# A whole program's instruction order, fixed by a plan in the kernel instead of by the scheduler

## Chip, cores, metric

One core of a Trainium2 chip runs the kernel. The metric is the device time of one execution in microseconds (us). The engines are the TensorE (PE in the profile; PEld is its weight load), the VectorE (DVE), the ScalarE (ACT), GpSimd (POOL) and the SyncE (SP), whose queue issues the DMA transfers.

## What is computed

The reference is a trunk of two layers over 512 tokens of width 1024. Each layer is a feed-forward part, a mixer and another feed-forward part:

```python
x = x + 0.5 * swiglu_ffn(rmsnorm(x, ffn1_norm[l]), ffn1_w_in[l], ffn1_w_out[l])
h = rmsnorm(x, mix_norm[l])
u_rwkv, u_gla, u_xa, u_gate = split_cols(h @ w_in[l], (RWKV_COLS, GLA_COLS, XA_WIDTH, GATE_COLS))
y_rwkv, v_first = rwkv7_mixer(u_rwkv, v_first, ...)
y_gla = gla_mixer(u_gla, gla_conv[l], gla_a_up[l], gla_a_bias[l], gla_norm[l])
y_xa = memory_attention(u_xa, rmsnorm(mem, mem_norm[l]), xa_w_kv[l])
branches = jnp.stack([y_rwkv, y_gla, y_xa], axis=2)
gates = jax.nn.sigmoid(u_gate.reshape(b, s, N_BRANCH, d))
merged = jnp.einsum('bsjc,jcd,bsjd->bsd', branches, w_branch[l], gates)
x = x + merged @ w_out[l]
x = x + 0.5 * swiglu_ffn(rmsnorm(x, ffn2_norm[l]), ffn2_w_in[l], ffn2_w_out[l])
```

The RWKV-7 mixer has 8 heads of width 64 and a state that each token updates: `state * w + sa * (kk * a) + v * k`, read out by `r`; its output is normalised per head, gets a bonus term and is multiplied by a gate. The gated linear attention has 4 heads in chunks of 64 tokens. The memory attention has 4 heads of width 128 over 256 memory rows.

## The kernel before

**Products.** Activations lie with features on the 128 partitions and the 512 tokens along the free axis. Every large product is made of three matmuls in fp32r for each 128 rows of its depth (`mm3`, L194 to L198; L307 in the mixer): weight and activation are split into a high and a low part, and high·high, high·low and low·high are summed in PSUM. Weights come from DRAM as `wraw` (L191, three buffers); the ScalarE rounds them to `whi` (L180), the VectorE makes `wlo` as the difference (L181). PSUM has three buffers `ps_b` for large products, and `ps_f` (one), `ps_i` (two), `ps_c` (one) and `ps_y` (one) for small ones. All small products are plain fp32.

**Stages of a layer.** The first feed-forward part (L262), then `mix` (L999): `xa_proj` projects the memory to keys and values, `norm_mix` (L218) makes the normalised `h` (`xn` at L226, its split `xhi`, `xlo` at L203 and L204); two of the four cross-attention heads; two pairs of GLA heads (`gla_pair`, which waits at L905 for the decays `gq` of L901); then the RWKV part; then branch 0, `w_out` (L1054 to L1061) and the second feed-forward part.

**The RWKV part** works on four pairs of heads (`hp`) by two halves of the tokens (`hf`), eight units in all. A unit consists of `rwkv_gates` and `rwkv_first` (vectors, masked products `MA` and `A4`, L459 and L472), `rwkv_inverse` (a triangular inverse by doubling, products `X` at L539 and `W` at L547 in turn), `rwkv_second` (the recurrence over chunks: L590 gives `qs`, L596 gives `VU`, L602 gives the new state `S`, and at the end L618 gives `y`) and `rwkv_out` (statistics of `y` down to L650, L655, the gate at L656, the result at L663 or L666). The last pair of heads leaves its result in `y3`, which branch 0 needs. The small products of these steps are a chain over TensorE, VectorE and ScalarE; the large products of the gates and branches, and of cross-attention heads 2 and 3, are put between them.

**What sets the order.** A scheduler that comes with the language orders all engines by priority, the program's order being the default. Two places differ. In `weave` (L670 to L778) the TensorE's order is written by hand (L1046): each part is a generator that yields the cost of the products it has just issued and the time until its next step is ready, and a loop takes the first part in a fixed list that is ready, or else a piece of the large products; all other engines are still left to the scheduler there, and the parts run under a raised priority. And `norm_mix` has a priority that is raised over everything else (L1011).

Of the kernel before, what the change touches and what calls it, by code (L numbers as in the profile page):

```python
# [19 lines left out]
P = 128  # L20
# [58 lines left out]

class Net:  # L80
    def __init__(self, ctx, tc, I):
        self.tc, self.nc, self.I = tc, tc.nc, I
        self.ctx = ctx
# [9 lines left out]
    def pool(self, name, bufs, ctx=None, **k):  # L93
        return (ctx or self.ctx).enter_context(self.tc.tile_pool(name=name, bufs=bufs, reuse_waits="tile", **k))
# [99 lines left out]
    def mm3(self, ps, a, b, start, stop):  # L194
        nc = self.nc
        nc.tensor.matmul(ps, a[0], b[0], start=start, stop=False)  # L196
        nc.tensor.matmul(ps, a[0], b[1], start=False, stop=False)  # L197
        nc.tensor.matmul(ps, a[1], b[0], start=False, stop=stop)  # L198

# [95 lines left out]
    @staticmethod  # L295
    def drain(g):
        while True:
            try:
                next(g)
            except StopIteration as e:  # L300
                return e.value

    def pieces(self, ps, w, xs):
        n = len(w)
        for k in range(n):
            for i, (a, b) in enumerate(((0, 0), (0, 1), (1, 0))):
                self.nc.tensor.matmul(ps, w[k][a], xs[k][b], start=k + i == 0, stop=k == n - 1 and i == 2)  # L307
                yield 227

    def proj_g(self, i):  # L310
        w = self.weight(self.I["w_main"][self.l, i], KD, P)
        ps = self.big()
        yield from self.pieces(ps, w, self.h)
        return ps

    def proj(self, i):
        return self.drain(self.proj_g(i))

    def shifted_g(self, i, out):

        nc = self.nc
        ps = yield from self.proj_g(i)
# [3 lines left out]

    def shifted(self, i, out):
        self.drain(self.shifted_g(i, out))
# [21 lines left out]
    def rwkv_rkv(self, hp):  # L350
# [16 lines left out]
        yield from self.shifted_g(4 + hp, k)  # L367
        r = self.lr.tile([P, T], F32, name="rk_r", tag="rk_r", bufs=1)
        yield from self.shifted_g(hp, r)
# [4 lines left out]

    def rwkv_gates(self, hp, hf, wz, r, k, v):
# [3 lines left out]
        if hf == 0:  # L381
# [5 lines left out]
            yield 0, 1800  # L387
# [22 lines left out]
        yield (2 * 432 if hf else 4 * 432), 6500  # L410
        return r, k, v, kk, kh, a, G

    def rwkv_first(self, hp, hf, r, k, v, kk, kh, a, G):
# [30 lines left out]
        yield 218, 4000  # L444
# [36 lines left out]
        self.freed = 2 * hp + hf + 1  # L481
        yield 8 * 218, 3600
# [23 lines left out]
        out = E, AR, VU, u0, GR, Z  # L506
        yield 8 * 116 + 432, 2800

        self.inv[2 * hp + hf] = Z, AB, AU, W32

        while self.tails < 2 * hp + hf - 1:
            yield None
# [5 lines left out]
        yield 4 * 109, 1000  # L518
# [4 lines left out]
        yield 432, 1000  # L523
        self.sec[2 * hp + hf] = (*out, KBT, bv)

    def rwkv_inverse(self, Z, AB, AU, W32):
# [8 lines left out]
        for b in (4, 8, 16):  # L535
# [8 lines left out]
            yield 4 * 216, 1000  # L544
# [4 lines left out]
            yield 4 * 216, 1300  # L549
# [12 lines left out]
        yield 432, 2100  # L562
# [8 lines left out]
        yield 432, 1300  # L571

    def rwkv_second(self, hp, hf, E, AR, VU, u0, GR, Z, KBT, bv):
# [4 lines left out]
        for c in range(4):  # L578
# [9 lines left out]
            else:  # L588
# [4 lines left out]
                yield 218, 650  # L593
# [5 lines left out]
            yield 218, 900  # L599
            if g < 7:  # L600
# [9 lines left out]
                if c < 3:  # L610
                    yield 218, 1000
# [12 lines left out]
        self.out[2 * hp + hf] = y, bv  # L624
        yield 5 * 218, 0

    def rwkv_out(self, hp, hf, y, bv):
# [23 lines left out]
        yield 0, 11000, 100000  # L651
# [16 lines left out]
        yield 218 + 432, 1500  # L668

    def weave(self, rkv0, gl, restore, xa):  # L670


        now, slack = 0, 400
        ready, rkv, gated, query = {0: 6000}, {0: rkv0}, {}, {}
        self.inv, self.sec, self.out, inverted = {}, {}, {}, 0
        self.freed = self.seconds = self.tails = 0

        def first_gates():
            for n in range(8):
                while n // 2 not in rkv or ready[n // 2] > now or self.freed < n:  # L680
                    yield None
                gated[n] = yield from self.rwkv_gates(n // 2, n % 2, *rkv[n // 2])

        def first():
            for n in range(8):
                while n not in gated or self.seconds < n - 1:
                    yield None
                yield from self.rwkv_first(n // 2, n % 2, *gated.pop(n))

        def inverse():  # L690
            nonlocal inverted
            for n in range(8):
                while n not in self.inv:
                    yield None
                yield from self.rwkv_inverse(*self.inv.pop(n))
                inverted = n + 1

        def second():
            for n in range(8):
                while n not in self.sec or inverted <= n or self.tails < n - 1:  # L700
                    yield None
                yield from self.rwkv_second(n // 2, n % 2, *self.sec.pop(n))
                self.seconds = n + 1

        def outputs():
            for n in range(8):
                while n not in self.out:
                    yield None
                yield from self.rwkv_out(n // 2, n % 2, *self.out.pop(n))
                self.tails = n + 1  # L710

        def heads():
# [445 lines left out]
```

## Time and profile before

| | us |
|---|---|
| median of three runs | 2859.72 (2856.72 to 2859.89) |
| the profiled execution | 2855.2 |
| its span in the profile | 2853.4 |
| TensorE busy | 2750.2 |
| VectorE, ScalarE busy | 1573.8, 1164.4 |

The profile is of one execution. A row of the view of waits names the engine, tile and line that waited, after the arrow what it waited for, and then the microseconds in all, the number of waits and the longest. In a row of the timeline stand start, length, engine, line, operation, output<-inputs, partitions x elements, a count of instructions taken together, and in brackets the idle time before it and what ended it. The TensorE's fp32 products are recorded as two instructions each.

### The profile page before, as it was taken

What the parts mean: (1) busy time and instruction counts of PE and PEld (TensorE: products, weight loads), DVE (VectorE), ACT (ScalarE), POOL (GpSimd) and SP (SyncE); (2) the same over time, 40 slices, a digit from 0 to 9 for tenths busy, and PEclk for the clock granted to TensorE, in tenths of its full rate; (3) what the DMA queues carried; (4) which work ended last, traced back from release to release, by engine and by line L of the source; (5) the groups of instructions that cost most, each with busy time, mean ns of one, the idle gap of its engine ahead of it and who ended that gap; (6) DMA issues with size and microseconds to landing.
All of it is one profiled execution on the core that took longest, in us unless ns stands there. A gap on an engine that the chain in (4) does not pass through costs nothing.

```text
span 2853.4 us, 35385 instructions
## 1 busy us (share of the span) xinstructions
PE 2750.2 (96%) x13280; PEld 2253.1 (79%) x13280; DVE 1573.8 (55%) x3057; ACT 1164.4 (41%) x2154; POOL 19.6 (1%) x102
## 2 busy tenths in 40 slices
PE   8999999999989999999999999999999999999998
PEld 6888877777777888888888888777777788888886
DVE  6434445677776555444554444555777665544443
ACT  5323345555443343323443233464544433432332
POOL 0000000000000000000000000000000000000000
PEclk9999999999989999999999999999999899999999
DMA  5232332211111332222332223312211113322222
GB/s 188 87 104 98 105 118 74 97 61 54 53 60 49 105 121 96 91 102 92 105 107 92 101 96 122 112 59 94 65 54 54 52 58 107 118 96 94 99 94 83
DMA packets 91723, 258.04 MB, mean 90 GB/s; under 512 B 10464, under 2 KB 24832, under 8 KB 91552
## 3 DMA queue, kind: packets, MB, share of 16 engines
q1 hardware_dynamic: 91552, 255.79, 26.4%
q8 instruction: 104, 1.70, 0.2%
q14 instruction: 67, 0.55, 0.1%
HBM read 243.69 MB, written 12.06 MB: 90 GB/s over the span
## 4 chain that ended last, share of the span: by engine, by line
PE 88%; DVE 7%; ACT 3%; issue 2%; DMA 0%; SPq 0%; DVEq 0%; ACTq 0%
PE ps_b L307 21%; PE ps_b L198 18%; PE ps_b L196 18%; PE ps_b L197 18%; PE ps_c L539 1%; PE ps_c L547 1%; DVE wlo L181 1%; PE ps_i L454 1%; PE ps_f L596 1%; PE ps_f L820 1%; PE ps_f L842 1%; ACT whi L180 0%; PE ps_i L392 0%; PE ps_y L956 0%; PE ps_i L925 0%
## 5 line engine op out<-in xcount | busy, mean ns | idle before, releaser
L180 ACT ACTIVATE whi<-wraw 128x512 fp32r<-128x512 f32 (+1 forms) x874 | 543.5, 622 | 1186.5 <-PE ps_b L197 912.3
L181 DVE TENSOR_TENSOR wlo<-wraw,whi 128x512 fp32r<-128x512 f32 (+1 forms) x874 | 590.6, 677 | 585.0 <-ACT whi L180 573.9
L196 PE MATMUL ps_b<-xhi,whi 128*128 128x512 f32 x1424 | 555.9, 390 | 8.9 <-ACT xhi L206 7.7
L198 PE MATMUL ps_b<-xhi,wlo 128*128 128x512 f32 x1424 | 555.6, 390 | 0.8 <-DVE wlo L181 0.8
L197 PE MATMUL ps_b<-xlo,whi 128*128 128x512 f32 x1424 | 555.6, 390 | 0.0
L307 PE MATMUL ps_b<-xhi,wlo 128*128 128x512 f32 x864 | 353.9, 410 | 7.4 <-DVE wlo L181 7.4
L307 PE MATMUL ps_b<-xhi,whi 128*128 128x512 f32 x864 | 353.4, 409 | 2.2 <-DVE wlal L325 1.7
L307 PE MATMUL ps_b<-xlo,whi 128*128 128x512 f32 x864 | 353.9, 410 | 0.0
L196 PEld LDWEIGHTS ps_b<-xhi,whi 128*128 128x128 f32 x1424 | 266.3, 187 | 66.8 <-ACT xhi L206 7.7
L198 PEld LDWEIGHTS ps_b<-xhi,wlo 128*128 128x128 f32 x1424 | 266.4, 187 | 58.9 <-DVE wlo L181 1.6
L197 PEld LDWEIGHTS ps_b<-xlo,whi 128*128 128x128 f32 x1424 | 266.4, 187 | 57.6 <-DVE xlo L207 0.5
L196 PE MATMUL ps_b<-mhi,whi 128*128 128x512 f32 x704 | 277.5, 394 | 0.0
L198 PE MATMUL ps_b<-mhi,wlo 128*128 128x512 f32 x704 | 276.0, 392 | 0.0
L197 PE MATMUL ps_b<-mlo,whi 128*128 128x512 f32 x704 | 273.3, 388 | 0.0
L307 PEld LDWEIGHTS ps_b<-xhi,wlo 128*128 128x128 f32 x864 | 165.6, 192 | 41.5 <-DVE wlo L181 9.9
L307 PEld LDWEIGHTS ps_b<-xhi,whi 128*128 128x128 f32 x864 | 165.6, 192 | 39.0 <-issue 5.3
L307 PEld LDWEIGHTS ps_b<-xlo,whi 128*128 128x128 f32 x864 | 165.8, 192 | 32.0 <-issue 2.6
L198 PEld LDWEIGHTS ps_b<-mhi,wlo 128*128 128x128 f32 x704 | 132.1, 188 | 30.9
L197 PEld LDWEIGHTS ps_b<-mlo,whi 128*128 128x128 f32 x704 | 132.2, 188 | 29.5
L196 PEld LDWEIGHTS ps_b<-mhi,whi 128*128 128x128 f32 x704 | 132.4, 188 | 26.3
L283 DVE TENSOR_TENSOR fm<-ps_b,ft 128x512 f32<-128x512 f32 x88 | 60.9, 692 | 127.2 <-PE ps_b L198 127.2
L279 DVE TENSOR_TENSOR ft<-ps_b,rs 128x512 f32<-128x512 f32 x88 | 60.9, 692 | 126.1 <-PE ps_b L198 125.9
(299 smaller groups left out, 3274.1 us busy)
## 6 DMA issues: line engine op xcount, KB each, us to landing
wraw<-in_ffn_in_dram SPq DMA_DIRECT2D x176, 512.0 KB, 3.4
wraw<-in_w_main_dram SPq DMA_DIRECT2D x108, 512.0 KB, 3.4
wraw<-in_ffn_out_dram SPq DMA_DIRECT2D x64, 512.0 KB, 3.5
wraw<-in_ffn_out_dram SPq DMA_DIRECT2D x64, 192.0 KB, 2.3
wraw<-in_w_branch_dram SPq DMA_DIRECT2D x48, 256.0 KB, 2.6
wraw<-in_w_out_dram SPq DMA_DIRECT2D x16, 512.0 KB, 3.4
xd<-x SPq DMA_DIRECT2D x16, 256.0 KB, 2.2
wraw<-in_w_k_dram SPq DMA_DIRECT2D x8, 512.0 KB, 3.6
```

The source lines that it names most:

```text
L180: nc.scalar.activation(hi, r, AF.Copy)
L181: nc.vector.tensor_tensor(lo, r, hi.bitcast(F32), ALU.subtract)
L196: nc.tensor.matmul(ps, a[0], b[0], start=start, stop=False)
L197: nc.tensor.matmul(ps, a[0], b[1], start=False, stop=False)
L198: nc.tensor.matmul(ps, a[1], b[0], start=False, stop=stop)
L279: nc.vector.tensor_tensor(t, pp[0], rs, ALU.mult)
L283: nc.vector.tensor_tensor(m, pp[1], t, ALU.mult)
L307: self.nc.tensor.matmul(ps, w[k][a], xs[k][b], start=k + i == 0, stop=k == n - 1 and i == 2)
L454: nc.tensor.matmul(pss[j][:, c * P:(c + 1) * P], KBc[js, c, :], AR[js, c, :], start=True, stop=True)
L539: nc.tensor.matmul(ps[:, u, :], AB[:, u, :], X[:, u, :], start=True, stop=True)
L547: nc.tensor.matmul(ps[:, u, :], W[:, u, :], Z[:, u, :], start=True, stop=True)
L596: nc.tensor.matmul(psu[:, :P], Z[:, 2 * p:2 * p + 2, :].rearrange("p j t -> p (j t)"), qs, start=True, stop=True)
```

## The change

The scheduler is no longer used. Around the unchanged arithmetic a recorder takes the place of the engines: each call is kept as an operation with the parts of tiles that it reads and writes, from which its dependences follow, and a cost by formula. After the whole program is recorded, `plan` lays it out in time six times and keeps the layout with the earliest end; `issue` then issues all instructions of all engines in the order of that layout, under a manual schedule.

In the layout, the TensorE takes of its ready operations a small product before a large one and else follows the order of the program. The other engines take the one whose latest start, counted back from what the TensorE needs, is earliest; the ScalarE avoids a change of its function table. A dependence costs a hop of 34 ns, and toward the TensorE 150 + 120 ns more (400 for 150 after a DMA).

```diff
+class Recorder:
+    ENGINES = ("tensor", "vector", "scalar", "gpsimd", "sync")
...
+    HOP, SLACK = 34, 150
+    def lag(self, p, o, slack=True):
+        if o.engine is None:
+            return 0
+        if p.engine == o.engine == "tensor":
+            return None
+        if p.engine == o.engine and p.engine != "sync":
+            return self.HOP
+        s = (400 if p.engine == "sync" else self.SLACK) if slack and o.engine == "tensor" else 0
+        return self.HOP + s + (120 if o.engine == "tensor" else 0)
...
+        def key(o):
+            return (o.kind, o.n) if o.engine == "tensor" else (late[o], o.n)
...
+                if e == "scalar":
+                    best = min(ready[e], key=lambda q: q[0] + (2000 if q[-1].table not in (None, table) else 0))
...
+    def plan(self, passes=6):
...
+        late = {o: float(o.n) for o in self.ops}
+        best = None
+        for _ in range(passes):
+            order = self.run(late)
+            end = max(o.start + o.took for o in order if o.engine == "tensor")
+            if best is None or end < best[0]:
+                best = end, order, {o: o.start for o in order}
+            late = self.urgency(order)
+        self.end, order, self.at = best
+        return order
```

The costs are formulas by engine and kind; the VectorE's, with those of two slow operations:

```diff
+            if o.what == "reciprocal":
+                o.took = 130 + 6.3 * n
+            elif o.what == "tensor_tensor_scan":
+                o.took = 139 + 2.11 * n
+            elif o.what == "memset":
+                o.took = 60 + n / 0.96
+            else:
+                fast = o.what in ("tensor_scalar", "tensor_copy") and not psum
+                o.took = ((n / 2 if fast else n) + 151) / 0.96 + (55 if col and o.what != "tensor_tensor" else 0)
+            o.busy = max(o.took - 80, 60)
```

`mm3` marks its three matmuls as large (`nc.kind = 1`). The generators become plain functions (`proj_g`, `pieces` and `drain` to `product` and `proj`; `gate_g` and `branch_g` to `gate` and `branch`), and `weave` with its ready times is replaced by a list of units and a list of large pieces of which a number is recorded behind each unit:

```diff
-    def weave(self, rkv0, gl, restore, xa):
...
+    def rwkv_fill(self, rkv, fill):
+        todo, made, done = list(fill), 0, None
+        share = [0, 5, 5, 5, 5, 5, 5, 4, 4]
+        for n in range(9):
+            if n < 8:
+                hp, hf = divmod(n, 2)
+                if n > 0 and hf == 0:
+                    rkv = self.rwkv_rkv(hp)
+                now = self.rwkv_first(hp, hf, *self.rwkv_gates(hp, hf, *rkv))
+                self.rwkv_inverse(*now[1])
+            if done is not None:
+                m = n - 1
+                self.rwkv_out(m // 2, m % 2, *self.rwkv_second(m // 2, m % 2, *done))
+            done = now[0] if n < 8 else None
+            for _ in range(share[n]):
+                if todo:
+                    todo.pop(0)()
+        for f in todo:
+            f()
...
-            with self.tc.high_priority(offset=100000):
-                self.h = self.norm_mix()
+            self.h = self.norm_mix()
...
-                with self.tc.manual_schedule(engines={mybir.EngineType.PE}):
-                    gates = self.weave(rkv, (yh, yl), lambda: restore(self.yx), (xp, kT, vm))
...
+                fill = [part(head, 2)] + [part(self.branch, 1, m, yh, yl, True) for m in range(2)] + [part(head, 3)]
+                fill += [part(self.branch, 1, m, yh, yl, True) for m in range(2, KD)]
+                fill += [part(second_branch, m) for m in range(KD)]
+                self.rwkv_fill(rkv, fill)
...
-            rs, rt = self.rstd(mt, NMEM, D)
+            rs, rt = self.rstd(mt, NMEM, D, copy=False)
...
-            Net(ctx, tc, ins).run(out)
+            net = Net(ctx, tc, ins)
+            net.run(out)
+            net.nc.issue(net.nc.plan())
```

The edit of `rstd` lets the memory norm read its scale from PSUM and saves one VectorE copy; all other instructions are the same. As every instruction is now issued from one line of the recorder, the rows of the changed order all have line L278. In the rows below, engine by engine, stand line, operation, output<-inputs and the output's shape; the numbers behind the names tell buffers apart and differ between the kernels.

The VectorE in the memory projection of layer 0, before: `xn` and `xlo` belong to `norm_mix`, `wlo` and `kT` to the projection.

```order
L226 SCALAR_TENSOR_TENSOR xn_3121<-x2_85,par0_78,ps_f_3108 128x512
L226 SCALAR_TENSOR_TENSOR xn_3125<-x3_86,par0_78,ps_f_3108 128x512
L793 TENSOR_TENSOR kT_2837<-ps_b_2920,rsm_1101 128x256
L204 TENSOR_TENSOR xlo_3076<-xn_3121,xhi_3075 128x512
L204 TENSOR_TENSOR xlo_3076<-xn_3125,xhi_3075 128x512
L226 SCALAR_TENSOR_TENSOR xn_3129<-x4_87,par0_78,ps_f_3108 128x512
L226 SCALAR_TENSOR_TENSOR xn_3133<-x5_88,par0_78,ps_f_3108 128x512
L181 TENSOR_TENSOR wlo_2953<-wraw_2946,whi_2952 128x512
```

The same place of the VectorE now:

```order
L278 TENSOR_TENSOR wlo_3045<-wraw_2937,whi_3033 128x512
L278 SCALAR_TENSOR_TENSOR xn_3052<-x2_87,par0_79,ps_f_2968 128x512
L278 SCALAR_TENSOR_TENSOR xn_3062<-x3_93,par0_79,ps_f_2968 128x512
L278 TENSOR_TENSOR wlo_3070<-wraw_2937,whi_3055 128x512
L278 TENSOR_TENSOR xlo_3006<-xn_3052,xhi_2993 128x512
L278 TENSOR_TENSOR kT_2947<-ps_b_3036,rsm_415 128x256
L278 TENSOR_TENSOR wlo_3090<-wraw_2983,whi_3080 128x512
L278 TENSOR_TENSOR xlo_3006<-xn_3062,xhi_2993 128x512
L278 TENSOR_TENSOR wlo_3100<-wraw_2983,whi_3092 128x512
L278 SCALAR_TENSOR_TENSOR xn_3107<-x4_99,par0_79,ps_f_2968 128x512
L278 TENSOR_TENSOR wlo_3114<-wraw_3041,whi_3103 128x512
```

Five `wlo` stand between the norm's instructions where one stood behind seven others.

The TensorE at the end of the RWKV part of layer 0, in the recurrence of the last unit, before:

```order
L590 MATMUL ps_y_7664<-S1_107,AR_7128 128x128
L307 MATMUL ps_b_7658<-yh_6717,wlo_7655 128x512
L307 MATMUL ps_b_7658<-yh_6717,whi_7654 128x512
L307 MATMUL ps_b_7658<-yl_6718,whi_7654 128x512
...
L596 MATMUL ps_f_7673<-qs1_109,Z_7191 128x128
```

And now, down to the product that takes the finished `y`:

```order
L278 MATMUL ps_f_7999<-qs1_91,Z_7737 128x128
L278 MATMUL ps_f_8003<-VU_7378,KBT_7750 128x128
L278 MATMUL ps_y_8007<-S0_95,AR_7657 128x128
L278 MATMUL ps_f_8011<-qs0_85,Z_7737 128x128
L278 MATMUL ps_f_8015<-VU_7378,KBT_7750 128x128
L278 MATMUL ps_y_8019<-S1_89,AR_7657 128x128
L278 MATMUL ps_f_8023<-qs1_91,Z_7737 128x128
L278 MATMUL ps_y_8026<-VU_7378,GR_7705 128x128 x4
L278 MATMUL ps_f_8056<-cst_133,y_7899 128x128 x2
L278 MATMUL ps_f_8056<-sgl_2916,g2_221 128x256
L278 MATMUL ps_b_7927<-yh_7220,whi_7768 128x512
```

The large products between the steps of this recurrence stand elsewhere. Before, 51 of them stood between the product of `VU` and `GR` and the one that takes `y`; now there is none.

The TensorE in cross-attention head 2 of layer 0 now: transposes of `pr`, products of `pt`, and scores from `kT` and `xq`, for the two halves of the tokens.

```order
L278 MATMUL ps_f_5245<-cst_133,pr_5228 128x128 x4
L278 MATMUL ps_f_5255<-pt_5251,vm_3185 128x256 x2
L278 MATMUL ps_f_5261<-kT_2947,xq_4619 128x256 x2
L278 MATMUL ps_f_5273<-cst_133,pr_5267 128x128 x4
L278 MATMUL ps_f_5280<-pt_5278,vm_3185 128x256 x2
L278 MATMUL ps_f_5287<-kT_2947,xq_5285 128x256 x2
L278 MATMUL ps_b_5290<-xhi_2993,whi_5144 128x512
```

Before, 13 to 21 large matmuls stood between such scores and the transposes that follow on them; here there are none in this head.

More of the change, by code (lines that the diff above doesn't have):

```diff
@@ L292, in ffn, with product, shifted @@
                     nc.vector.scalar_tensor_tensor(self.x[o], ps, 0.5, self.x[o], ALU.mult, ALU.add)
[L295 to L311, printed above, removed]
+    def product(self, w, xs):
         ps = self.big()
[L313 removed]
+        for k, (a, b) in enumerate(zip(w, xs)):
+            self.mm3(ps, a, b, k == 0, k == len(w) - 1)
         return ps
     def proj(self, i):
[L317 to L319 removed]
+        return self.product(self.weight(self.I["w_main"][self.l, i], KD, P), self.h)
+    def shifted(self, i, out):
         nc = self.nc
[L322 removed]
+        ps = self.proj(i)
         nc.gpsimd.memset(out[:, 0:1], 0.0)
```

506 lines of the change are left out of this document (348 added, 158 removed).

## The prediction

> **What bounds the kernel now.** I read the page from the top, then the busy time by stretches, then the waits of the TensorE, then the order of time in the stretches where it waits.
>
> ```profile
> span 2853.4 us, 35385 instructions
> PE 2750.2 (96%) x13280; PEld 2253.1 (79%) x13280; DVE 1573.8 (55%) x3057; ACT 1164.4 (41%) x2154; POOL 19.6 (1%) x102
> PE 88%; DVE 7%; ACT 3%; issue 2%; DMA 0%; SPq 0%; DVEq 0%; ACTq 0%
> ```
>
> The TensorE is busy for 2750.2 of 2853.4 us and is 88% of the chain that ended last. So 103.2 us are idle TensorE, and everything else that can be won lies in matmuls that run slower than they could. The change leaves the matmuls as they are; it can only move these two. Where they lie, by stretches (columns: stretch, length, busy time and count of PE, PEld, DVE, ACT, POOL, granted clock, DMA share, GB/s):
>
> ```profile
> 50.00:372.00 322.00, 322.00 (x1421) 265.91 (x1420) 145.67 (x224) 106.04 (x169) 0.00 (x0) 1.00 0.30 101
> 372.00:405.00 33.00, 27.73 (x159) 24.27 (x159) 22.07 (x37) 15.30 (x25) 1.25 (x8) 0.84 0.31 108
> 470.00:506.00 36.00, 30.48 (x169) 24.20 (x168) 21.13 (x37) 18.71 (x26) 0.00 (x0) 0.81 0.09 30
> 560.00:932.00 372.00, 342.95 (x2032) 284.02 (x2031) 261.75 (x697) 173.68 (x420) 6.87 (x33) 0.96 0.16 55
> 1778.00:1812.00 34.00, 28.72 (x164) 25.28 (x163) 22.80 (x38) 15.30 (x25) 1.25 (x8) 0.85 0.36 123
> 1877.00:1912.00 35.00, 29.45 (x166) 23.43 (x165) 21.13 (x37) 18.05 (x25) 0.00 (x0) 0.80 0.08 30
> 1975.00:2350.00 375.00, 345.43 (x1996) 283.55 (x1996) 267.19 (x700) 177.12 (x424) 6.88 (x33) 0.96 0.17 56
> ```
>
> The first row is the feed-forward: no idle time, clock 1.00, a 128x512 matmul each 322.00/1421 = 0.227 us. Nothing can be won there, and the same holds for the other feed-forward stretches. The rest come in pairs, one for each layer: the memory projection (xa_proj with norm_mix, 5.27 + 5.28 us idle), the gated linear attention (5.52 + 5.55), and the RWKV weave (29.05 + 29.57). The clock is below one in just these stretches. What they wait for:
>
> ```profile
> PE ps_f L655 <- DVE y L650: 20.9, 10, 3.0
> PE ps_i L905 <- DVE gq L901: 9.3, 3, 4.6
> PE ps_b L307 <- DVE wlo L181: 7.4, 4, 2.9
> PE ps_f L596 <- DVE sg L666: 7.4, 4, 2.6
> PE ps_b L197 <- DVE wlo L181: 6.0, 2, 3.0
> ```
>
> The VectorE is what ends most waits, though it is only 262/372 = 70% busy in the weave: the trouble is the order in which it does things, and the distance on the TensorE between a matmul and the one that needs what the VectorE makes of it.
>
> **The change, part by part.** All instructions but one VectorE copy stay; only positions move.
>
> *Memory projection.* In order of time, layer 0:
>
> ```profile
> 390.02 1.40 DVE L226 SCALAR_TENSOR_TENSOR xn<-x,par,ps_f 128x512 f32<-128x512 f32 x2
> 391.94 1.28 DVE L204 TENSOR_TENSOR xlo<-xn,xhi 128x512 fp32r<-128x512 f32 x2
> 392.07 0.38 PE L198 MATMUL ps_b<-yh,wlo 128*128 128x256 f32 x1 [2.27 <-DVE wlo L181]
> 393.14 1.39 DVE L226 SCALAR_TENSOR_TENSOR xn<-x,par,ps_f 128x512 f32<-128x512 f32 x2
> 395.05 1.29 DVE L204 TENSOR_TENSOR xlo<-xn,xhi 128x512 fp32r<-128x512 f32 x2 [0.18 <-ACT xhi L203]
> 396.26 1.89 DVE L181 TENSOR_TENSOR wlo<-wraw,whi 128x512 fp32r<-128x512 f32 x3
> 397.00 0.80 PE L197 MATMUL ps_b<-wlo,yh 128*128 128x512 f32 x1 [3.00 <-DVE wlo L181]
> 398.44 0.63 PE L198 MATMUL ps_b<-whi,yl 128*128 128x512 f32 x1
> ```
>
> The wlo, which the running matmuls need, stands behind xn and xlo of the norm, which are needed only later: 2.27 + 3.00 = 5.27 us, all the idle time of the stretch. After that the matmuls run at half rate: from 397.00 to 398.44 four of them start (two between are not shown), 1.44 us less the first one's 0.59 leaves 0.43 each, against 0.227. The granted clock agrees: 0.16 of 33 us = 5.3 us of clock lost, of which the part beyond the wait itself is some 3.5. In the changed order wlo and xn alternate on the VectorE, a wlo first. Both waits go, and their half clock with them: −(5.3 + 3.5) × 2 = **−17.5**.
>
> [...]
>
> *Gated linear attention.* The same chain of 4.6 us stays in front of L905; 31 instead of 34 large matmuls stand in it, so it waits 3 × 0.227 = 0.7 us longer in each layer: **+1.4**.
>
> *Start.* The program's first weight load is issued here:
>
> ```profile
> 2.12 0.43 SPq L191 DMA_DIRECT2D wraw<-in_ffn_in_dram  x1
> ```
>
> Three loads stand before it on the queue; now it is first. I give this **−2**, with bounds 0 (x, not the weight, sets the start) and −2.1 (all of it).
>
> *RWKV weave, what a step needs.* The recurrence, at a place where little else runs on the VectorE:
>
> ```profile
> 927.60 0.38 PE L602 MATMUL ps_f<-VU,KBT 128*128 128x128 f32 x2
> 928.02 0.57 DVE L608 SCALAR_TENSOR_TENSOR S<-S,E,ps_f 64x64 f32<-64x64 f32 x2 [2.25 <-PE ps_f L602]
> 929.45 0.38 PE L590 MATMUL ps_y<-S,AR 128*128 128x128 f32 x2
> 929.87 0.28 DVE L591 TENSOR_TENSOR qs<-ps_y,u 64x128 f32<-64x128 f32 x1 [0.20 <-PE ps_y L590]
> 930.83 0.38 PE L596 MATMUL ps_f<-qs,Z 128*128 128x128 f32 x2
> 931.49 0.22 ACT L598 ACTIVATE VU<-ps_f 64x64 f32<-64x64 f32 x1
> 932.45 1.05 PE L618 MATMUL ps_y<-VU,GR 128*128 128x128 f32 x8
> 933.60 0.85 DVE L623 TENSOR_TENSOR y<-ps_y,y 64x256 f32<-64x256 f32 x2
> 939.60 0.42 DVE L650 TENSOR_TENSOR y<-y,rt 128x256 f32<-128x256 f32 x1
> ```
>
> From the start of L590 to the end of qs 0.70, from L596 to the end of VU 0.88, from L602 to the end of S 0.99; with 0.06 for the hop that is 0.76, 0.93 and 1.05 us that the TensorE must fill from one to the next. From the last L618 (about 933.2) to the end of y 6.8 us: with the hop, 6.9.
>
> In the order of before, every step has more than it needs (medians: 1.36, 1.58, 1.76, and 11.3 to 14 for y, worked out from the order as the matmuls between, 0.227 a large one and 0.22 a small product). So its 58.6 us of waits are not missing distance; they are a VectorE that is busy with something else. In the changed order the plan has placed the VectorE's instructions too, and the distances have shrunk nearly to the need: 0.9, 0.9, 1.1 to 1.3, and 6.5 to 10 for y. I count what is short, over both layers:
>
> - The last half's recurrence stands with no large matmul between its steps: six steps of each layer are short by 0.73, 0.83, 0.56, 0.73, 0.83, 0.56 = 4.24; two layers 8.5, elsewhere 1.9: 10.4.
> - y of the last half: nothing between L618 and L655, 6.8 short, twice; others 1.4: 15.0.
> - Branch 0 behind it needs y3, and only nine large matmuls that do not need it are left, 2.0 us. From L656 to y3 it takes 2.5 us, and the split into two halves another 1.3 and a wait, so about 2.8 short, twice: 5.6.
>
> ```profile
> 923.23 0.60 PE L656 MATMUL ps_f<-sgl,g 128*128 128x256 f32 x2
> 925.35 0.42 DVE L663 TENSOR_TENSOR y<-t,ps_f 128x256 f32<-128x256 f32 x1
> ```
>
> - Cross-attention heads 2 and 3: scores, transposes and values stand nearly back to back in head 2. From the last of the four score matmuls (about 431.65) to the transposes it takes 3.7 us at the undisturbed place below; the distance is 0.43 and 2.7 (1.11 and 3.16 in the other layer) instead of 5 to 8. Short 7.8, and 3.0 at the values: 10.8.
>
> ```profile
> 430.96 1.13 PE L820 MATMUL ps_f<-kT,xq 128*128 128x256 f32 x4
> 434.83 0.62 DVE L830 TENSOR_SCALAR pr<-pr,mx 128x256 f32<-128x256 f32 x2
> 435.33 0.30 PE L836 MATMUL ps_f<-cst,pr 128*128 128x128 f32 x1
> ```
>
> - The masked products: from the last L454 to the inverse's first matmul two MA and two A must run, 0.4 + 2 × 0.42 + 2 × 0.42 = 2.1 to 2.2 us; the distance is now 1.2 to 1.9, in all 16 halves short by 10.5 together (1.0 more later in the inverse).
>
> ```profile
> L459 DVE TENSOR_TENSOR MA<-ps_i,cst 128x256 f32<-128x256 f32 x32 | 13.2, 417 | 10.2 <-PE ps_i L454 9.8
> L472 DVE TENSOR_TENSOR A<-MA,cst 64x256 f32<-64x256 f32 x32 | 13.4, 420 | 0.5
> ```
>
> Sum 53.3 against 58.6: **−5.3**. The half clock of the weave was 0.04 × 372 + 0.04 × 375 = 29.9 us of lost clock, of which some 20 fell on running matmuls; the new waits are gathered at the end and at the heads, about 14: **−6**. The bounds: if the plan's VectorE is as late as before's wherever slack is gone, the 58.6 come on top of the 53.3 (no gain, +53); if the gaps counted overlap each other, none but the tail's (8.5 + 13.6 + 5.6 = 28) are left: −31, and −9 of half clock more.
>
> *Hidden in it.* Waits too short to be named (about 15 us in each weave, what the matmuls of that stretch take over 0.227 each) I leave as they are; the 15 is an estimate and in no sum but that of the first rival.
>
> Sum: −17.5 + 1.4 − 2 − 5.3 − 6 = **−29** on the profiled execution's 2855.2: 2826. The median of the runs, 2859.7, lies 4.5 above that execution, so 2830.
>
> **The rivals.**
>
> *The plan holds in full.* The waits of the weave overlap as in the lower bound, and the hidden ones go as well: −40 and part of −30. For it: one plan knows all five engines, and the prices written into it agree with the rows (it takes 151/0.96 + 256/0.96 = 424 ns for L472, measured 420). Against: it forces 6.8 us of plain gap at the end of each weave. About 2800.
>
> *The end of the weave costs more.* While y's chain of small instructions runs with nothing on the TensorE, the splits of branch 0's weights and other VectorE work stand between them: up to 33 instead of 15 us. About 2848.
>
> *Tight steps slip (slower).* Place: the recurrence and the inverse, 11 steps of one and 12 of the other in a half, 23 × 16 = about 360. Price: each has 0 to 0.25 us of slack left where before had 0.6 to 0.7, and a VectorE instruction from elsewhere that stands ahead of it takes 0.42 to 0.69. If one step in four meets half of one or more, 0.15 us a step, 54 us are lost: −29 + 54 = +25, 2884. It decides from 29/360 = 0.08 us a step. For it: the fixed order cannot give way when an engine is late, on any engine now; the waits for L650 and L666 show what a late VectorE costs even with slack. Against: in the trace a small instruction's time repeats to a few hundredths, so a plan made of such times slips little.
>
> *The change does nothing.* The order differs on every engine, so only by sums that cancel; that is inside the chances below.
>
> **How the numbers follow.** Forecast 2830: 0.42. Full plan 2800: 0.20. Costly end 2848: 0.17. Tight steps 2884: 0.21. The last one is spread from 2850 on (0.08 us a step is break-even), so part of it, and the edge of the third, makes "no change". The runs of this kernel differ by about 0.1%, so 0.2%, 5.7 us, is taken as the least that can be told. Faster (under 2854) 0.72, same 0.09, slower (over 2865.4) 0.19. The range reaches from a little below the second case to the nearer half of the last: 2790 to 2872. The forecast's own range is 2812 to 2846.
>
> **What would show it.** In the memory projection the VectorE's wlo must not end a wait over 1 us, and the granted clock there must be near 1.00; otherwise the first term is wrong. The matmul that takes y into ps_f must wait once for nearly 7 us in each layer, right behind eight products of VU and GR, and not for 20.9 us in ten places. The products of pr must wait in head 2, and those of A in each half for 0.3 to 1.0. If the slower case is right, the products of S, qs and VU and those of X and W carry many waits of 0.1 to 0.5 us each, and the weave takes more than its 372 us; if it takes under 350, the full plan holds. If the idle time of the weave falls and its length does not, the clock has taken it back. The forecast is wrong if the feed-forward stretches, which are given nothing here, move by more than a few us: the plan orders them too, and a late wlo there would cost 0.7 us each time.

## The result

The changed kernel takes 2857.5 us (median of 12 runs, 2854.7 to 2867.5), the kernel before 2858.2 (12 runs, 2854.8 to 2862.4). The ratio is 1.0002, 95% interval 0.9992 to 1.0012: no difference that can be measured, where 2830 was forecast. The profiled execution of the changed kernel, 2867.5 us, is its slowest; a second trace, of an execution of 2855.5 us, stands beside it below.

The page of the first trace, its span, busy times and chain:

```profile
span 2865.7 us, 35465 instructions
PE 2775.7 (97%) x13280; PEld 2257.5 (79%) x13280; DVE 1575.8 (55%) x3056; ACT 1167.4 (41%) x2150; POOL 19.8 (1%) x102
PE 92%; DVE 5%; ACT 2%; issue 1%; DMA 1%; DVEq 0%; ACTq 0%; SPq 0%
```

Idle TensorE fell from 103.2 to 90.0 us, and its busy time rose by 25.5 us, for the same 13280 matmuls. So the waits went and the matmuls became slower, or waits went where "busy" hides them. The stretches, first the memory projection (columns as before: PE, PEld, DVE, ACT, POOL, granted clock, DMA share, GB/s):

```profile
372.00:405.00 33.00, 33.00 (x199) 27.64 (x198) 24.70 (x42) 18.77 (x32) 1.25 (x8) 1.00 0.46 167
1785.00:1818.00 33.00, 33.00 (x199) 27.60 (x198) 24.70 (x42) 18.75 (x32) 1.25 (x8) 1.00 0.47 175
```

No idle time, clock 1.00. The linear attention and, behind it, all up to the first product of `w_out`; first the kernel before, then the changed one in the first and in the second trace:

```profile
462.00:573.00 111.00, 104.31 (x544) 83.03 (x544) 67.46 (x111) 60.78 (x87) 0.30 (x3) 0.94 0.23 81
573.00:1015.00 442.00, 412.97 (x2297) 341.95 (x2297) 299.94 (x761) 199.59 (x467) 6.87 (x33) 0.97 0.19 66
1869.00:1983.00 114.00, 108.32 (x553) 83.39 (x554) 68.14 (x112) 61.49 (x88) 0.30 (x3) 0.94 0.23 79
1983.00:2431.00 448.00, 418.43 (x2303) 343.65 (x2302) 306.51 (x769) 203.29 (x471) 6.88 (x33) 0.97 0.20 65
```

```profile
452.00:576.00 124.00, 112.86 (x552) 90.01 (x551) 68.93 (x111) 60.66 (x86) 0.20 (x2) 0.88 0.21 73
576.00:1021.00 445.00, 421.23 (x2288) 338.23 (x2287) 299.75 (x761) 201.84 (x465) 7.07 (x34) 0.97 0.19 65
1865.00:1995.00 130.00, 118.87 (x557) 91.38 (x557) 69.25 (x112) 61.54 (x88) 0.20 (x2) 0.87 0.21 69
1995.00:2444.00 449.00, 425.44 (x2298) 340.37 (x2297) 307.05 (x769) 204.88 (x469) 7.07 (x34) 0.97 0.19 65
```

```profile
452.00:569.00 117.00, 105.28 (x556) 83.95 (x557) 69.77 (x111) 60.54 (x86) 0.30 (x3) 0.96 0.23 77
569.00:1014.00 445.00, 421.34 (x2289) 338.32 (x2287) 299.75 (x764) 202.17 (x465) 6.94 (x33) 0.97 0.21 66
1858.00:1983.00 125.00, 113.86 (x541) 87.85 (x540) 68.82 (x111) 59.47 (x86) 0.30 (x3) 0.88 0.21 70
1983.00:2432.00 449.00, 424.26 (x2311) 340.02 (x2310) 307.26 (x769) 206.35 (x472) 6.94 (x33) 0.98 0.21 65
```

The linear attention is longer by 6 to 16 us in each layer; its clock is 0.87 or 0.88 for 0.94 in three of the four cases, and 0.96 in the one that is longer by 6 us. The weave has less idle time (24 for 29 us in each layer) and is no shorter: its busy time rose by as much. And the waits of the first trace (all have line L278 now, so the tiles tell them apart):

```profile
PE ps_f L278 <- DVE y L278: 13.7, 8, 5.8
PE ps_i L278 <- DVE gq L278: 12.7, 2, 6.4
PE ps_f L278 <- ACT xq L278: 6.8, 3, 3.2
PE ps_f L278 <- DVE pr L278: 4.9, 2, 2.8
PE ps_b L278 <- ACT yh L278: 4.6, 2, 2.3
```

With the stages cut at the same matmuls in each trace (starts from the timeline, both layers added, up to the last matmul), the account is:

| stage | before | changed, second trace | difference | forecast |
|---|---|---|---|---|
| start to the first memory product | 376.9 | 376.2 | −0.7 | −2 |
| memory projection | 66.5 | 48.2 | −18.3 | −17.5 |
| heads 0 and 1 | 103.4 | 103.2 | −0.2 | 0 |
| linear attention, up to its first product that needs gq | 27.3 | 29.5 | +2.2 | +1.4 |
| linear attention, the rest | 198.6 | 214.8 | +16.2 | 0 |
| weave and branch 0 | 889.3 | 891.6 | +2.3 | −11.3 |
| w_out, feed-forward, end | 1182.3 | 1181.1 | −1.2 | 0 |

In the first trace the linear attention's rest is at +25.9 and the weave at +4.5; the other rows agree within 0.4. In both, six large products of each layer have moved from the weave into the linear attention (1.4 us each way).

### The profile page after: what moved, and what is told of

The parts are those of the page before. It is cut to its first block, busy times and chain, and to the rows that moved or that the text cites. A ratio compares the mean times of both kernels' runs of the same rounds, so it can differ in the third digit from the quotient of the medians.

```text
span 2865.7 us, 35465 instructions
## 1 busy us (share of the span) xinstructions
PE 2775.7 (97%) x13280; PEld 2257.5 (79%) x13280; DVE 1575.8 (55%) x3056; ACT 1167.4 (41%) x2150; POOL 19.8 (1%) x102
## 4 chain that ended last, share of the span: by engine, by line
PE 92%; DVE 5%; ACT 2%; issue 1%; DMA 1%; DVEq 0%; ACTq 0%; SPq 0%
PE ps_b L278 78%; PE ps_i L278 4%; PE ps_f L278 4%; PE ps_c L278 3%; PE ps_y L278 2%; DVE y L278 1%; DVE wlo L278 1%; ACT whi L278 0%; DMA x<-in_x_dram 0%; DVE Z L278 0%; ACT L278 0%; DVE st L278 0%; ACT VU L278 0%; DVE tt L278 0%; DVE t L278 0%
## 5 line engine op out<-in xcount | busy, mean ns | idle before, releaser
L278 ACT ACTIVATE whi<-wraw 128x512 fp32r<-128x512 f32 (+1 forms) x874 | 544.3, 623 | 1208.6 <-PE ps_b L278 1170.9
L278 PE MATMUL ps_b<-xhi,whi 128*128 128x512 f32 x2288 | 911.8, 399 | 16.3 <-ACT whi L278 9.7
L278 PE MATMUL ps_b<-xlo,whi 128*128 128x512 f32 x2288 | 906.7, 396 | 0.3 <-DVE xlo L278 0.3
L278 PE MATMUL ps_b<-xhi,wlo 128*128 128x512 f32 x2288 | 905.5, 396 | 1.1 <-DVE wlo L278 1.0
L278 DVE TENSOR_TENSOR wlo<-wraw,whi 128x512 fp32r<-128x512 f32 (+1 forms) x874 | 590.7, 677 | 573.9 <-ACT whi L278 572.4
L278 PEld LDWEIGHTS ps_b<-xhi,whi 128*128 128x128 f32 x2288 | 431.5, 189 | 112.0 <-ACT whi L278 11.6
L278 PEld LDWEIGHTS ps_b<-xhi,wlo 128*128 128x128 f32 x2288 | 430.9, 188 | 93.6 <-DVE wlo L278 3.9
L278 PEld LDWEIGHTS ps_b<-xlo,whi 128*128 128x128 f32 x2288 | 430.9, 188 | 92.9 <-issue 3.6
L278 PE MATMUL ps_b<-mhi,whi 128*128 128x512 f32 x704 | 277.4, 394 | 0.0
L278 PE MATMUL ps_b<-mhi,wlo 128*128 128x512 f32 x704 | 276.0, 392 | 0.0
L278 PE MATMUL ps_b<-mlo,whi 128*128 128x512 f32 x704 | 273.2, 388 | 0.0
L278 PEld LDWEIGHTS ps_b<-mhi,wlo 128*128 128x128 f32 x704 | 132.1, 188 | 31.0
L278 PEld LDWEIGHTS ps_b<-mlo,whi 128*128 128x128 f32 x704 | 132.2, 188 | 29.6
L278 PEld LDWEIGHTS ps_b<-mhi,whi 128*128 128x128 f32 x704 | 132.3, 188 | 26.3
L278 DVE TENSOR_TENSOR fm<-ps_b,ft 128x512 f32<-128x512 f32 x88 | 60.9, 692 | 127.7 <-PE ps_b L278 127.6
L278 DVE TENSOR_TENSOR ft<-ps_b,rs 128x512 f32<-128x512 f32 x88 | 60.9, 692 | 122.7 <-PE ps_b L278 122.5
L278 PE MATMUL ps_b<-yh,whi 128*128 128x512 f32 (+1 forms) x256 | 96.8, 381 | 4.6 <-ACT yh L278 4.6
L278 PE MATMUL ps_b<-yl,whi 128*128 128x512 f32 (+1 forms) x256 | 98.2, 384 | 0.0
L278 PE MATMUL ps_b<-yh,wlo 128*128 128x512 f32 (+1 forms) x256 | 97.1, 379 | 0.0
L278 DVE SCALAR_TENSOR_TENSOR x<-ps_b,x 128x512 f32<-128x512 f32 x64 | 44.3, 692 | 61.1 <-PE ps_b L278 61.0
L278 DVE TENSOR_TENSOR ft<-ft,rs 128x512 f32<-128x512 f32 x88 | 61.0, 693 | 13.5 <-ACT ft L278 5.4
```

Of the source, the lines that this page charges most:

```text
L278: return getattr(getattr(self.tc.nc, engine), what)(*(f(v) for v in a), **{n: f(v) for n, v in k.items()})
```

## The experiments

Three places are to be told apart: the linear attention, the weave's waits that no view names, and the waits that the plan itself makes at head 2 and at the end of the weave.

**The gain of the memory projection by itself.** In the kernel before, one edit:

```diff
-            with self.tc.high_priority(offset=100000):
-                self.h = self.norm_mix()
+            self.h = self.norm_mix()
```

> The kernel before with one edit: norm_mix loses its raised priority, so that wlo may stand ahead of xn and xlo on the VectorE in the memory projection. In the changed kernel this stretch fell from 33.3 to 24.1 us in each layer. Theory A (that gain is real and is independent of the rest): the stretch falls to 24 to 26 us in each layer, and the time by 15 to 18 us, to about 2842; the changed kernel then lost as much elsewhere. Rival (the gain is given back at once, since norm_mix is late for the products behind it): the stretch is shorter but the next one longer by as much, and the time stays within 4 us of 2858.

2860.0 us, ratio 1.0011 (1.0000 to 1.0021): the rival. The stretch fell from 33.3 to 22.2 us in each layer, and the next, up to the first scores, rose from 12.4 to 20.8 and 21.6. The timeline of layer 0 shows where:

```profile
403.38 2.08 PE L254 MATMUL ps_f<-cst,rt 128*128 128x128 f32 x8 [1.78 <-DVE rt L251]
406.96 0.61 PE L196 MATMUL ps_b<-xhi,whi 128*16 128x512 f32 x1 [1.50 <-ACT xhi L203]
```

The scheduler now does the norm last: its own products wait for the statistics, and the first product that needs `h` waits for `xhi`, at the half clock again. The priority was no mistake. The plan interleaves the two streams instruction by instruction, and in the changed kernel the next stretch stays at 12.6 us; that no simpler order would do is not shown.

**The linear attention: the gap.** The decays of the first pair are recorded ahead of heads 0 and 1, so that the chain from `aup` to `gq` runs under their products.

```diff
                     al = self.gla_al(gp)
+                    decay = self.gla_decay(gp, 0, al)
                     head(0)
                     head(1)
-                    self.gla_pair(gp, 0, al, yh, yl)
+                    self.gla_pair(gp, 0, al, yh, yl, decay)
```

> The changed kernel with the decays of the first GLA pair recorded ahead of cross-attention heads 0 and 1, so that the first kh transposes no longer wait 6.4 us for them. The linear attention (from the first product of al and aup to the last of qz and St) took 123.9 and 130.2 us in the changed kernel, 30.7 and 34.1 us in all at the half clock there. Theory A (the gap sets off the half clock, and everything at half rate behind it follows from it): gap and half clock go, -12.8 for the waits and -22 to -24 for the clock, time about 2857 - 30 = 2822 to 2830. Rival B (small products nearly alone on the TensorE pull the clock down by themselves): the gap goes, but half rate stays over some 17 us or more in each layer, time 2838 to 2848. Rival C (the products that filled heads 0 and 1 are now short there): the waits move to the heads, time within 5 us of 2857.

2829.0 us (2827.9 to 2830.3), ratio 0.9901 (0.9888 to 0.9914): theory A. No wait for gq is left, and from the first product of `aup` to the last of `St` the clock is 0.99:

```profile
407.00:558.00 151.00, 147.15 (x755) 117.14 (x754) 88.49 (x154) 88.50 (x138) 0.20 (x2) 0.99 0.26 84
```

Some half clock is left in this trace behind other waits, 3.4 us in layer 0 and 6.8 in layer 1. And the edit does not close the gap alone: of the first 124 matmuls from the transposes of `gq` on, 31 are large here and 4 in the changed kernel, so a denser mix is a rival that this run leaves (e3_mix below tries the mix without closing the gap). It does show one thing of small products: in the second half of the pair 82 matmuls, 4 of them large, ran at full clock, so these 10 us of small products did not by themselves bring it down.

```profile
460.10:470.00 9.90, 9.75 (x82) 7.38 (x81) 4.68 (x12) 4.13 (x8) 0.00 (x0) 1.00 0.27 98
```

The spread of the runs, 12.8 us in 12 runs of the changed kernel, is 2.4 in 4 runs here.

**The linear attention: large products among the small.**

```diff
+                    if pick[0] == 0 and pick[-1].mix and small >= 4:
+                        pick = min((q for q in ready[e] if q[0] == 1), default=pick)
```

> The changed kernel, the gap of 6.4 us left as it is, but in the linear attention the plan takes one large product after every four small ones, as the kernel before had (14 large ones among the small ones of the second half of the first pair, 2 in the changed kernel, 15 here). Theory A' (after a gap, small products nearly alone keep the clock at half): the half clock behind the gap falls from 30.7 and 34.1 us to 10 to 17 us as before, -8 to -12 us in each layer in its profile, time 2835 to 2842. Rival (the length of the gap, 6.4 against 4.5 us, keeps the clock down): the half clock stays at 27 to 34 us, time within 4 us of 2857.

2873.3 us, ratio 1.0062 (1.0046 to 1.0078): slower, which neither expected. The half clock behind the gap is shorter in its trace (13.7 us and twice 3.4, for 30.7 and 34.1), but the stage is not (110.7 and 115.4 us for 109.1 and 115.4): at full rate the spacing of its matmuls grew by 9 us in the two layers, 4 of them idle time and 2.7 for six more large products of each layer that the plan took out of the weave, and took it back. As the next run shows, such a length differs between executions by itself, so this run doesn't settle what ends the half clock. Its runs, 2866.5 to 2883.0 us, go with the granted clock: 0.979 in the traced one, 0.973 in the slowest.

**A second trace of the changed kernel.**

> The changed kernel as it is, for a second trace, since its first profiled execution (2867) lies 10 us above its median (2857). If the half clock of the linear attention (30.7 and 34.1 us in the first trace) is what differs between executions, an execution near the median shows 10 to 25 us in it for each layer and all stages else within 2 us of the first trace. Rival (the spread lies in the weave or elsewhere): the linear attention shows 28 to 35 us again.

2855.5 us. The first expectation holds for layer 0 and the rival for layer 1. The clock in the stretch behind the gap, in the first trace and then in the second:

```profile
464.00:494.00 30.00, 27.19 (x124) 22.25 (x125) 13.26 (x29) 10.10 (x14) 0.00 (x0) 0.50 0.00 1
```

```profile
465.20:475.20 10.00, 8.54 (x36) 7.25 (x36) 5.74 (x12) 2.92 (x5) 0.00 (x0) 0.50 0.00 0
475.60:496.00 20.40, 17.86 (x124) 14.30 (x124) 13.34 (x22) 13.54 (x17) 0.00 (x0) 1.00 0.08 27
1868.20:1898.50 30.30, 27.21 (x124) 22.28 (x125) 13.56 (x29) 10.38 (x14) 0.00 (x0) 0.50 0.00 1
```

The same instructions in the same order run at half rate for 30 us once and for 10 us the other time, which makes 8 us of this stage (109.1 against 101.1) and most of the 12 us between the two traces. In the kernel before the half clock at this place took 10.2 us in both layers, and in e1_prio, with the same order of the TensorE there and a gap of 4.3 us, 20.5 us in both (its traced run is its slowest).

**The weave: tight steps.** More distance in the plan.

```diff
-    HOP, SLACK = 34, 150
+    HOP, SLACK = 34, 400
```

> The changed kernel with SLACK 400 ns for 150 in the plan: every product stands a quarter of a us further behind what it needs. Theory B (tight steps: in the weave the waits below the recorded length of a matmul, counted as busy, grew by some 21 us over both layers): these shrink by 12 to 20 us, the named waits stay, time 2838 to 2846. Rival (what grew is not waiting but the mix of small and large products, which costs the same wherever it stands): time within 4 us of 2857, or later, since large products are used up sooner.

2865.6 us, ratio 1.0035 (1.0023 to 1.0047). Theory B is right in the size of what it took out, and the rival in the time; the named waits did not stay, as theory B had it (y 21.6 us for 13.7, pr 10.7 for 4.9). I compared, at full clock, the distance of each two successive matmuls with the shortest usual one for the same pair of shapes; what is over, less the named waits, is waiting that the modelled ends of matmuls cover. In the two weaves it is 89 us in the kernel before, 108 in the changed one, 93 here. How large they are depends on what is taken as the shortest usual distance; that they grow, by 19 to 26 us, and fall again, by 15 to 17, does not. But the weave is longer by 7 and 8 us, with idle time of 33 for 24 us and a clock of 0.95 and 0.94:

```profile
567.00:1019.00 452.00, 418.71 (x2288) 341.86 (x2287) 301.89 (x761) 201.71 (x465) 6.97 (x34) 0.95 0.20 64
1985.00:2442.00 457.00, 424.28 (x2295) 344.85 (x2295) 308.21 (x770) 206.75 (x471) 6.91 (x34) 0.94 0.20 64
```

Every step that is moved apart uses large products up, and they are missing where nothing else is left: at head 2 and at the end. So these two were tried next, on the kernel of e2_decay_early. In the changed kernel they look like this (timeline of layer 0, the head and then the end of the weave):

```profile
672.72 1.08 PE L278 MATMUL ps_f<-cst,pr 128*128 128x128 f32 x4 [2.78 <-DVE pr L278]
...
679.08 0.60 ACT L278 ACTIVATE xq<-ps_b 128x512 f32<-128x512 f32 x1 [2.10 <-DMA yx<-xq]
679.73 2.07 PE L278 MATMUL ps_f<-kT,xq 128*128 128x256 f32 x4 [3.17 <-ACT xq L278]
...
969.75 1.92 PE L278 MATMUL ps_y<-VU,GR 128*128 128x128 f32 x8
977.43 0.66 PE L278 MATMUL ps_f<-cst,y 128*128 128x128 f32 x2 [5.77 <-DVE y L278]
...
981.25 1.65 PE L278 MATMUL ps_b<-yh,whi 128*128 128x512 f32 x3 [2.30 <-ACT yh L278]
```

At 679.08 the finished product of head 3's query leaves PSUM, after it has waited for head 2's result to go to DRAM out of the one buffer `xq`: till then it held one of the three `ps_b`. That the large products behind it could not start for this reason is read from the kernel and these rows; the next run moves head 3 away, and doesn't test the buffer by itself.

```diff
-                fill = [part(head, 2)] + [part(self.branch, 1, m, yh, yl, True) for m in range(2)] + [part(head, 3)]
+                fill = [part(head, 2)] + [part(self.branch, 1, m, yh, yl, True) for m in range(4)] + [part(head, 3)]
```

> The kernel of e2_decay_early (2829) with cross-attention head 3 recorded behind four products of branch 1 instead of two. In the changed kernel head 2 waits on xq, pr and pt for 13.8 us over both layers, with no large product ready, because head 3's product holds one of three PSUM buffers until head 2 has let go of the only xq. Theory C (those waits and the half clock behind them, some 4 us, are lost there): 10 to 16 us less, 2813 to 2819. Rival (the large products that now stand in the head are missing at the end of the weave): the waits go from the head, the y wait at the end grows by as much, time within 4 us of 2829.

2806.7 us, 22.3 less than e2_decay_early: theory C, and more than it said. The waits for xq and pr (6.8 and 7.0 us in e2_decay_early) stand in no row any more; those for y are 16.8 us, for 13.7, so a little was taken over by the end.

```diff
+                gates += [self.gate(0, m, self.mx.tile([P, T], F32, name="gs", tag="gs", bufs=2)) for m in (4, 5)]
                 yh, yl = restore(self.yd, self.y3)
```

> The kernel of e2_decay_early (2829) with the gate products 4 and 5 of branch 0 (48 large products, 10.9 us) recorded ahead of branch 0, so that they can stand between the last recurrence and its y: 27 and 20 large products there instead of none. Theory D (the end of each weave, a wait of 5.8 us for y and 2.3 us for yh and a half clock worth about 4 us, is a loss by want of large products): 18 to 26 us less, 2803 to 2811; the wait for y at the end below 1 us and no half clock in the 20 us after it. Rival (the products are only moved, and branch 0 then waits instead): within 4 us of 2829.

2806.5 us, 22.5 less than e2_decay_early: theory D in the time. All waits for y are 3.6 us together, the longest 1.2. The waits for yh, which it counted in, stay (4.4 us for 4.6), and in layer 1 a half clock of 6.8 us stands at the end of the weave, in layer 0 none.

> The edits of e5_head3_later and e6_gates45 together. If theories C and D hold and are independent, their gains add: 2829 - 13 - 22 = 2794 (2787 to 2803). If both draw on the same supply of large products, the gain is that of the larger one alone, 2805 to 2815.

2785.6 us (2784.7 to 2788.0), ratio to the kernel before 0.9747 (0.9732 to 0.9763). The gains add: 22.3 + 22.5 = 44.8, measured 43.5. The two weaves are 24 and 21 us shorter than in the changed kernel's first trace and at a clock of 1.00 and 0.99:

```profile
557.00:978.00 421.00, 413.06 (x2293) 333.56 (x2292) 300.00 (x761) 201.44 (x464) 6.96 (x34) 1.00 0.21 69
1934.00:2362.00 428.00, 418.44 (x2294) 333.96 (x2294) 306.19 (x769) 204.41 (x469) 6.97 (x34) 0.99 0.22 68
```

**Slack again, with large products left.** SLACK 200 for 150 on e7_head_gates.

> e7_head_gates with SLACK 200 ns for 150. Slack of 400 took 15 us of waits hidden in the busy time out of the weave, but lengthened it since large products ran short at its end. Theory B with that shortage mended: 3 to 8 us less than e7_head_gates. Rival (the shortage is still what decides): 0 to 8 us more than e7_head_gates.

2781.5 us (2780.1 to 2782.1), 4.0 less than e7_head_gates, as theory B has it: with large products there to fill it, this distance paid. This is the fastest version, 2.7% below the kernel before (ratio 0.9733, 0.9715 to 0.9751). What it still waits for is, above all, 8.1 us at the program's start, and at the end of the weave of each layer 2.3 us for `y` (1.2 in e7_head_gates) and 2.3 us for `yh`:

```profile
PE ps_f L278 <- DVE y L278: 7.3, 8, 2.3
PE ps_b L278 <- ACT yh L278: 4.6, 2, 2.3
```

**Is the linear attention's gap independent of the rest, and of the plan?** First the edits of e7_head_gates without that of e2_decay_early.

> The edits of e7_head_gates on the changed kernel without that of e2_decay_early: the linear attention keeps its gap and half clock. If the three losses are independent, e7 without the 28 of e2: 2785 + 28 = 2813 (2807 to 2819). Rival (the loss in the linear attention comes from the supply of large products that the other two edits change): under 2800.

2805.0 us, 2 below the lower bound: the gap and what follows it cost 19.4 us here and not 28. In its trace the half clock behind the gap lasts 10.2 and 13.7 us, not 30, with the order of the TensorE in the first pair the same as in the changed kernel; so what e2_decay_early won was likely in part the longer half clock. That trace is of its fastest run (2801.5 us, clock 0.993); two of the four took 2807.7 and 2807.9 us at 0.989. The gap is a loss of its own either way. Then the edit of e2_decay_early in the kernel before.

> The kernel before, its scheduler unchanged, with the one edit of e2_decay_early: the decays of the first GLA pair recorded ahead of cross-attention heads 0 and 1. There the wait at L905 is 4.5 us in each layer and the half clock behind it costs 4.1 to 4.4 us. Theory A (gap and half clock are one loss, whoever sets the order): both go, 16 to 20 us less, 2837 to 2842. Rival (as with norm_mix in e1_prio, the scheduler gives it back in the next stretch): within 4 us of 2857.

2851.6 us (2845.0 to 2859.1), ratio 0.9983 (0.9971 to 0.9995): between the two. The waits of its trace, an execution of 2846.0 us:

```profile
PE ps_f L836 <- DVE pr L830: 5.3, 4, 1.6
PE ps_i L905 <- DVE gq L901: 4.3, 2, 2.2
PE ps_f L820 <- ACT xq L810: 4.3, 4, 1.3
```

The first pair is as theory A has it: in both layers its transposes of `gq` (at 457.5 and 1859.9 us) do not wait, and no half clock follows them.

```profile
455.00:470.00 15.00, 15.00 (x85) 12.07 (x83) 11.39 (x22) 10.28 (x19) 0.00 (x0) 1.00 0.25 77
```

The 4.3 us at L905 are new waits, 2.1 us in each layer, in front of the second pair (at 547.3 and 1954.5 us), and the heads wait longer (pr 5.3 for 2.0, xq 4.3 for 1.3 us): the scheduler gives a part back there. With the plan the same edit was worth 28 us.

## Why the forecast failed, step by step

- **Memory projection: right.** −17.5 forecast, −18.3 measured, and by the mechanism named: no wait, clock 1.00. That it is no matter of priority alone, e1_prio shows.
- **Linear attention: the step that failed most.** The prediction said that the chain stays and the wait grows by three large products, +1.4, and it had no term for the half clock behind the gap. The wait grew by 1.8 us in each layer (6.4 for 4.6). Of that 0.7 is the three large products, and 1.1 is the chain itself, which did not stay the same: from the product of `aup` to the start of the `gq` that is waited for it takes 14.0 us for 12.9. The ScalarE now does a `whi` ahead of two of its steps (timeline of the first trace; before, these steps stood 0.7 and 1.1 us closer behind `aup`):

```profile
454.84 0.63 ACT L278 ACTIVATE whi<-wraw 128x512 fp32r<-128x512 f32 x1 [0.94 <-PE ps_b L278]
455.38 0.62 ACT L278 ACTIVATE gE<-gE 128x512 f32<-128x512 f32 x1
...
460.25 0.63 ACT L278 ACTIVATE whi<-wraw 128x512 fp32r<-128x512 f32 x1 [1.79 <-PE ps_b L278]
460.90 1.28 ACT L278 ACT_TABLE_LOAD   x1
```

And the stage behind it grew by 16 us in the second trace and 26 in the first, 2.7 of them for the large products taken over from the weave. The rest is nearly all the length of the half clock, which was 31 to 34 us in three of four cases, for 10 before: in layer 0 of the second trace, where it is 10.2 us as before, the stage is longer by 3.2 us (101.1 for 97.9), in layer 1 with 30.7 us by 13.0 (113.7 for 100.8). e2_decay_early, with the gap closed, won 28 us. Why the half clock lasts so long stays open. Of the first 124 matmuls behind the gap 14 were large before and 4 are now, but e11_hg_no_early, with this same order and gap, shows 10.2 and 13.7 us, e1_prio, with the order of before, 20.5, and e3_mix, which put the large ones back, didn't show it in the time.
- **Weave, named waits: right in the sum, not in its parts.** 53.3 us forecast for 58.6; the idle time there is 48.4 in the second trace. The end is as foreseen, one wait of 5.8 us (6.8 forecast) and 2.3 for yh (2.8). Heads 2 and 3 wait longer, 13.8 us (xq, pr and pt) for 10.8. But of the 11.5 us that were put on the masked products and the inverse the first trace names 0.5 for `A` and 0.4 for `X`: that term failed, and the sum is near by luck. The half clock was forecast at 14 us; 29.5 us of the TensorE's busy time lie at half clock in the two weaves of the second trace, a loss of about 15.
- **Weave, hidden waits: failed.** "Waits too short to be named [...] I leave as they are" was an assumption, and it is the rival of the tight steps that took it: 108 for 89 us. Its estimate of 15 us in each weave does not come out of the row it points to (342.95 us over 2032 matmuls are 0.169 each, less than 0.227). From the windows the growth comes out alike: busy time rose by 845.6 − 831.4 = 14.2 us, though twelve large products fewer (2.7) and some 8 us less of half clock should have lowered it, 25 in all. Spread over the 368 steps that is 0.05 to 0.07 us, close under the 0.08 at which that rival was said to decide. The slack that the prediction measured as nearly gone was a cost, and the bound was there; the sum took it as zero.
- **Start: nearly nothing,** −0.7 for −2. The first weight load is issued at 0.75 us for 2.12, yet the first matmul waits 8.3 us in the first trace, for whi, where it waited 7.7 before, for xhi: an earlier weight load alone didn't start it sooner.

Together: linear attention 17 us above the forecast, weave 14 above it, the start 1, less 2 elsewhere: 30, the whole way from the 2826 forecast for the profiled execution to the 2855.5 of the second trace.

## What to carry to other kernels

A planner that packs the other engines removes waits that a profile names, and can pay in waits too short to be named, as here; where all distances are cut to the need, price the slack that is gone for every step. Filler work is a stock: count what is left where the dependent chain ends, and look at which buffer a finished product holds while it waits, since that may stop the filler though there is enough of it. A gap is worth closing beyond its own length when the clock falls behind it: here 6.4 us in each layer cost 19 to 28 us in all.

## What the runs showed of the hardware

The half clock behind the same gap and the same instructions lasted 10 us in one execution and 31 us in another, so 8 us of a stage are chance. The spread of the runs of the planned kernels went with the gap: 12.8 us in 12 runs of the changed kernel and 6.4 in 4 of e11_hg_no_early with it, 2.0 to 4.1 us in the five versions without it (4 runs each).

In the stretch of 30 us 120 of 124 matmuls are small products; they fill 91% of it and did not bring the clock back. At full clock, 10 us of such products (82 matmuls, 4 of them large, in e2_decay_early) did not bring it down.

By the clock records of the first trace of the changed kernel, the stretches at half rate up to the end of the second weave lasted 30.72, 13.65, 17.07, 34.13, 3.41, 10.24 and 17.07 us: 9, 4, 5, 10, 1, 3 and 5 times the shortest of them. Their starts at 671.80, 968.76 and 1876.71 us lie 61, 148 and 414 times 3.413 us behind the one at 463.59. In the kernel before, half rate began 0.7 us after the end of a wait of only 2.27 us, at 392.8, and with the end of another as long, at 1799.1 us.
